# Splitting each 128x1024 unit of weights with one cast and one subtraction instead of two halves each

## The chip, the cores and the metric

The kernel runs on one core of one Trainium2 chip. The metric is the device time of one execution in microseconds: 1812.07 us is the median of three runs (1810.32, 1812.13 and 1812.07). All times below are microseconds unless marked ns. The engines are PE (TensorE's matmuls) and PEld (its weight loads), DVE (VectorE), ACT (ScalarE), POOL (GpSimd) and SP, which here only issues DMAs.

## The reference

The program is the forward pass of two stacked blocks on one sequence of 256 tokens with 1024 features. The first block has two layers: a SwiGLU feed-forward, a mixer, and a second feed-forward, each followed by a layer norm of the residual. Its mixer is a gated linear recurrence (RG-LRU) in layer 0 and a dilated attention with keys and values shared from the layer before in layer 1. The second block puts 16 meta tokens in front (272 tokens) and has two layers of a hybrid mixer (retention, pooling and a forgetting attention) and a SwiGLU feed-forward.

```
x = layer_norm(ALPHA*x + 0.5*swiglu(x, w_in, w_out))
x = layer_norm(ALPHA*x + mixer(x))          # rglru_block or dilated_attention
x = layer_norm(ALPHA*x + 0.5*swiglu(x, w_in2, w_out2))
...
h = layer_norm_2(ALPHA*h + mix @ w_out)     # second block, twice
h = layer_norm_2(ALPHA*h + (silu(h@w1) * (h@w3)) @ w2)
```

What matters here is that almost all of the time goes into matrix products of a 1024- to 2816-long input with large fp32 weights, each weight used once.

## The kernel before, in words

Activations lie transposed in SBUF: 128 features on the partitions, 256 or 272 tokens on the free axis. Every weight matrix is cut into 128x128 tiles, and the tiles lie in DRAM in the order in which the program uses them, eight to a unit of 128x1024 fp32 numbers (512 KB): 537 units. A product of full precision is made of three matmuls in the fast format fp32r (`mm3`, matmul at L147): weight and input are each split into a high part, rounded to fp32r, and a low part, the difference; the three matmuls are high x high, high x low and low x high. So each unit feeds 24 matmuls.

Three steps bring a unit to PE. `_dma` (L77) loads it into a raw buffer (five of them) from the queue of SP. `_hi` (L87) makes the high part on ACT, as two casts of 128x512. `_lo` (L99) makes the low part as two subtractions of 128x512, raw minus high; they run on DVE, but on POOL while `lo_pool` is set, which is so in the recurrence (`rg`). High and low parts have seven buffers each. `w` hands out the tiles one by one, and at the first tile of each unit `pump(2)` splits up to two more units, never more than six units ahead of the one in use.

DVE and ACT have other work between the splits: the evacuation of PSUM (L441 to L443 in the feed-forward), the splits of activations (L159 and L160), the residual and what the next norm needs (L252, L211, L215, L198), the norm itself (L272 to L300), and the mixers' own vector work: convolution, scans and gates in `rg` (L508 to L566), softmaxes, and the chain of the forget gates in the second block's mixer (L840 to L855). Norms are covered by `filler`: the first output tiles of the next stage are computed from the input that is not yet normalised, and put right afterwards.

The order of the instructions on each engine is fixed when the program is built. A scheduler walks the instructions in the order in which the code emits them, gives the engine that is free in its own estimate of time the earliest one that is ready, and assigns the semaphores. Blocks under `high_priority(offset=100)` (the residual, the statistics, the norm) are ranked as if emitted 100 instructions earlier. On the chip each engine then works through its list strictly in order. At the start, `body` splits the first two units between the splits of the first input tiles.

Of the kernel before, what the change touches and what calls it, by code (L numbers as in the profile page):

```python
# [57 lines left out]
class Builder:  # L58
# [12 lines left out]

    # ---------------------------------------------------------------- weights
    def _dma(self):
# [4 lines left out]
        self.raws[u] = raw  # L78

    def _hi(self):  # L80
        u = self.nhi
        while self.ndma < min(u + RAWS, N_UNIT):
            self._dma()
        self.nhi += 1
        hi = self.p_w.tile([128, UNIT * 128], F32R, tag="whi", name="whi")
        for q in range(0, UNIT * 128, 512):
            self.nc.scalar.copy(hi[:, q:q + 512], self.raws[u][:, q:q + 512])  # L87
        self.his[u] = hi

    def _lo(self, pool=False):  # L90
        u = self.nlo
        while self.nhi <= u:
            self._hi()
        self.nlo += 1
        lo = self.p_w.tile([128, UNIT * 128], F32R, tag="wlo", name="wlo")
        eng = self.nc.gpsimd if pool or self.lo_pool else self.nc.vector
        r, h = self.raws.pop(u), self.his[u].bitcast(F32)
        for q in range(0, UNIT * 128, 512):
            eng.tensor_tensor(lo[:, q:q + 512], r[:, q:q + 512], h[:, q:q + 512], op=ALU.subtract)  # L99
        self.los[u] = lo  # L100

    def pump(self, n, pool=False):
        """Splits up to n more units of weights, the high parts one unit ahead of the low parts."""
        u = self.used // UNIT
        while n > 0 and self.nlo < min(u + LOOK, N_UNIT):
            if self.nhi < min(self.nlo + 2, N_UNIT):
                self._hi()
            self._lo(pool)
            n -= 1
# [18 lines left out]

    # ---------------------------------------------------------------- helpers
    def bank(self, n=1, hold=None):  # L130
        """The next free psum bank (or aligned pair, or three in a row); a held one is skipped until it is let go."""
        b = self.bank_ptr
        for _ in range(16):
            b %= 8
            if (n == 2 and b % 2) or b + n > 8 or any(b + i in h for h in self.held.values() for i in range(n)):
                b += 1
                continue
            break
        else:
            raise AssertionError("no free bank")  # L140
        self.bank_ptr = (b + n) % 8
        if hold is not None:
            self.held[hold] = range(b, b + n)
        return self.ps[:, b, :] if n == 1 else self.ps[:, b:b + n, :]
# [23 lines left out]

    # ---------------------------------------------------------------- layer norm
    def ln_begin(self, ln, N):  # L170
# [3 lines left out]
    def emb_begin(self):  # L174
        """The columns and the meta tokens that the norm of all tokens adds to the first block's last one."""
        nc = self.nc
        nc.scalar.copy(self.gh[:, :, LTOT:LTOT + 4], self.exh.bitcast(F32))
        nc.scalar.copy(self.gl[:, :, LTOT:LTOT + 4], self.exl.bitcast(F32))
        t = self.p_ln.tile([128, LTOT], F32, tag="nt", name="nt", bufs=3)[:, 0:KD * META]
        t = t.rearrange("p (k n) -> p k n", k=KD)  # L180
        nc.vector.tensor_tensor(t, self.xf[:, :, 0:META], self.ex[:, :, 2:3].to_broadcast([128, KD, META]), op=ALU.mult)
        self.split(self.gh[:, :, 0:META], self.gl[:, :, 0:META], t)

    def sums(self, m, N, off, sq, eng, eng2=None):
        """Running sums of x and x^2 over the feature tiles."""
        a = self.acc
# [16 lines left out]
    def fold_to(self, m, ln, N):  # L203
        """Factor and columns of the next stage's first input."""
        if ln == LN_EMB - 1:
# [12 lines left out]
    def prep(self, ms, ln, N, off, fold=True):  # L218
        """What the next norm needs of the feature tiles ms, which end together."""
        nc = self.nc  # L220
# [23 lines left out]
    def scale_in(self, m, ln, N, off):  # L244
        """x <- x g, once the sums have what they need of it."""
        x = self.xf[:, m, off:off + N]
# [8 lines left out]
    def stats(self, N, eps, tail=None, dst=None):  # L255
        """Mean and deviation of every token from the running sums; tail: the last tile's share comes on top."""
        nc = self.nc
# [22 lines left out]
    def table(self, func, after):  # L280
        """Has ScalarE load the table set of func ahead of its use."""
        self.nc.scalar.activation(self.dummy, after, func)

    def norm(self, ln, N, off):
        """Normalises all feature tiles, software-pipelined over VectorE and ScalarE."""
        nc = self.nc
# [16 lines left out]
    def norm_last(self, ln, N, off, i, eng, rstd, nm):  # L303
        """Normalises a feature tile that scale_in has been over."""
        nc = self.nc
# [16 lines left out]
    def filler(self, specs, ln, N, off, eps, pool, tag="fv", bufs=2, when=(1, 3)):  # L322
        """First output tiles of a stage, from the not yet normalised input."""
        n = len(specs)
# [15 lines left out]
    def emb_filler(self, specs, eps_in, eps, pool, tag):  # L340
        """The first output tiles of the second block, from the first block's last sums: two norms are still to come.
        The first one is of the tokens without the meta tokens, the second one of all."""
        nc = self.nc
# [45 lines left out]
    def group(self, specs, N, kout=False, mid=None):  # L389
        """Output tiles in pairs from the normalised input; returns one [128, 2, N] psum view per pair.  # L390
        mid: what is emitted after the first half."""
        shared = 2 * N <= 512
# [15 lines left out]
    def out_proj(self, K, hh, hl, spec, coef, ln, N, off, fold, waves, korder=None, hooks={}):  # L408
        """x <- x + coef * (h @ W), in waves of output tiles; hooks: what is emitted amid the first wave."""
        if ln == LN_EMB - 1:  # L410
# [20 lines left out]

    # ---------------------------------------------------------------- feed forward
    def ffn(self, sg, su, so, coef, ln_in, ln_out, N, off, eps_in, fold_out=True):
# [24 lines left out]

    # ---------------------------------------------------------------- RG-LRU
    def rg(self, ln_in, ln_out, eps):  # L460
# [140 lines left out]

    # ---------------------------------------------------------------- shared keys and values
    def kv(self, ln_in, eps):
# [32 lines left out]

    # ---------------------------------------------------------------- dilated attention
    def attn(self, ln_in, ln_out, eps):
        nc = self.nc
        N, off = SEQ, META  # L640
        with self.tc.tile_pool(name="attn", bufs=1) as p:
# [20 lines left out]
            def put(pr, g, src):  # L662
                """High part of a head's queries in its own half of the partitions, low part in the other one."""
                for e in range(2):
# [69 lines left out]
            def step(n=1):  # L734
                """Head i's scores while the heads before it are a stage further each."""
                for _ in range(n):
# [35 lines left out]

    # ---------------------------------------------------------------- second block's mixer
    def mixer(self, l, ln_in, ln_out, eps, eps_in=None):
# [4 lines left out]
        with self.tc.tile_pool(name="mix", bufs=1) as p:  # L779
# [26 lines left out]

            # ---- projections of the forgetting attention
            six = l == 0
# [28 lines left out]
            nc.gpsimd.memset(one, 1.0)  # L837
            # log sigmoid of the forget logits and its running sum
            with self.tc.high_priority(offset=PRIO):
# [54 lines left out]

            # ---- forgetting attention, one head at a time
            S, DEN, PT, O = {}, {}, {}, {}
# [82 lines left out]

            # ---- retention  # L980
            SM = p.tile([128, N], F32, name="SM")
# [98 lines left out]

            # ---- multi-scale pooling
            ua = {}
# [36 lines left out]

            # ---- order of work  # L1120
            def pair(a, b, mid=None):
# [81 lines left out]

    # ---------------------------------------------------------------- whole program
    def dump(self, N, off):
# [109 lines left out]
def constants():  # L1315
    """Tables that depend on shapes alone."""
    f8 = np.float64
# [49 lines left out]
def feat(a):  # L1367
    """[..., n*128] -> [128, ... * n]"""
    a = np.asarray(a)
    return np.ascontiguousarray(a.reshape(-1, 128).T)  # L1370


def lay_out(inp, plan):
    """Inputs rearranged for the program: no arithmetic, only order (and zero padding)."""
    r = {}
# [66 lines left out]
```

## Time and profile before

| | |
|---|---|
| runs | 1810.32, 1812.13, 1812.07; median 1812.07 |
| profiled execution | span 1813.3 from first to last instruction; the page gives no time of its own outside of it |
| busy PE / PEld / DVE / ACT / POOL | 1741.0 / 1675.4 / 1272.0 / 1032.6 / 230.0 |
| casts of the weights, ACT L87 | 1074 of 128x512, 615.5 busy |
| subtractions, DVE L99 | 1032 of 128x512, 685.7 busy |
| subtractions, POOL L99 | 42 of 128x512, 63.3 busy |

Busy time is the union of an engine's instructions; "idle" names the time just before an instruction and what ended it. In a timeline, consecutive instructions of one kind are merged: start, length, count. The chain of waits goes back from the last instruction to what released each step, so an engine's share in it is the time that this engine held up the end. [...]

### The profile page before, as it was taken

Reading aid. Unit: us, or ns where it says so; the run is one execution under the profiler, and the core shown is the slowest. Engines: PE = TensorE matmul, PEld = TensorE weight load, DVE = VectorE, ACT = ScalarE, POOL = GpSimd, SP = SyncE. Lnnn points to the kernel's source line nnn. Section 1 sums busy time; section 2 is a strip of 40 time slices with the busy share of each in tenths; the row PEclk is TensorE's granted clock in tenths of the full one; section 3 lists DMA queues with packets and bytes.
Section 4 is the critical chain, followed back from the end, with each engine's and each line's share of the span. In section 5 each row is a group of like instructions: output and inputs, shape, how many; then the busy total and the mean of one; then the engine's idle time right before and its main releaser. Section 6 shows DMA issues by size and latency. Waiting matters only on the chain.

```text
span 1813.3 us, 34554 instructions
## 1 busy us (share of the span) xinstructions
PE 1741.0 (96%) x13558; PEld 1675.4 (92%) x13558; DVE 1272.0 (70%) x2399; ACT 1032.6 (57%) x2090; POOL 230.0 (13%) x266
## 2 busy tenths in 40 slices
PE   8999978999999999999999999799999999999997
PEld 8999977999999999977789999788999998899996
DVE  6666899966676666756668666897965569687653
ACT  6444666744465444644547445775744457575443
POOL 0001355000100001201120001320200030120001
PEclk9999988999999999968999999999999999999999
DMA  8555435565548555732225555433365554246550
GB/s 292 185 187 186 145 105 168 170 209 186 182 156 280 186 187 186 208 118 82 82 85 179 188 183 184 154 106 106 118 208 176 177 188 152 83 129 223 186 186 35
DMA packets 85372, 296.80 MB, mean 164 GB/s; under 512 B 10892, under 2 KB 14232, under 8 KB 84696
## 3 DMA queue, kind: packets, MB, share of 16 engines
q1 hardware_dynamic: 80216, 283.79, 47.1%
q0 software_dynamic: 1424, 7.38, 1.3%
q10 hardware_dynamic: 3568, 3.41, 0.6%
q8 instruction: 106, 1.74, 0.4%
q14 instruction: 58, 0.48, 0.1%
HBM read 290.24 MB, written 4.19 MB: 162 GB/s over the span
## 4 chain that ended last, share of the span: by engine, by line
PE 82%; DVE 11%; ACT 3%; issue 2%; DMA 1%; POOL 1%; DVEq 0%; SPq 0%; POOLq 0%; ACTq 0%
PE ps L147 81%; DVE wlo L99 3%; DMA KL<-kl 1%; PE ps L155 1%; ACT whi L87 1%; DVE uc L510 0%; DVE gl L300 0%; DVE T L561 0%; DVE xf L252 0%; POOL wlo L99 0%; DVE nt L291 0%; DVE gl L215 0%; POOL acc L193 0%; DVE rstd L277 0%; DMA raw<-in_wst_dram 0%
## 5 line engine op out<-in xcount | busy, mean ns | idle before, releaser
L87 ACT CAST whi<-raw 128x512 fp32r<-128x512 f32 x1074 | 615.5, 617 | 525.7 <-issue 311.0
L99 DVE TENSOR_TENSOR wlo<-raw,whi 128x512 fp32r<-128x512 f32 x1032 | 685.7, 701 | 321.5 <-ACT whi L87 319.6
L147 PE MATMUL ps<-gh,whi 128*128 128x256 f32 (+3 forms) x2864 | 829.0, 290 | 19.6 <-ACT gh L297 8.7
L147 PE MATMUL ps<-gl,whi 128*128 128x256 f32 (+3 forms) x2864 | 823.3, 288 | 1.0 <-DVE gl L300 1.0
L147 PE MATMUL ps<-gh,wlo 128*128 128x256 f32 (+3 forms) x2864 | 818.4, 286 | 0.0
L147 PEld LDWEIGHTS ps<-gh,whi 128*128 128x128 f32 x2864 | 549.3, 192 | 27.2 <-ACT gh L297 9.3
L147 PEld LDWEIGHTS ps<-gl,whi 128*128 128x128 f32 x2864 | 550.9, 192 | 5.9 <-issue 2.6
L147 PEld LDWEIGHTS ps<-gh,wlo 128*128 128x128 f32 x2864 | 551.1, 192 | 1.3 <-issue 0.7
L147 PE MATMUL ps<-hh,wlo 128*128 128x256 f32 (+1 forms) x1056 | 298.0, 282 | 0.0
L147 PE MATMUL ps<-hh,whi 128*128 128x256 f32 (+1 forms) x1056 | 297.9, 282 | 0.0
L147 PE MATMUL ps<-hl,whi 128*128 128x256 f32 (+1 forms) x1056 | 297.7, 282 | 0.0
L147 PEld LDWEIGHTS ps<-hl,whi 128*128 128x128 f32 x1056 | 199.0, 188 | 0.0
L147 PEld LDWEIGHTS ps<-hh,whi 128*128 128x128 f32 x1056 | 199.0, 188 | 0.0
L147 PEld LDWEIGHTS ps<-hh,wlo 128*128 128x128 f32 x1056 | 198.8, 188 | 0.0
L193 POOL TENSOR_TENSOR acc<-xf 128x256 f32<-128x256 f32 (+1 forms) x10 | 7.6, 759 | 1060.7 <-DVE xf L252 907.7
L443 DVE TENSOR_TENSOR th<-th,ps 128x512 f32<-128x512 f32 (+1 forms) x62 | 42.9, 691 | 54.3 <-PE ps L147 54.3
L193 POOL TENSOR_TENSOR acc<-acc,xf 128x256 f32<-128x256 f32 (+1 forms) x50 | 45.5, 910 | 192.3 <-DVE xf L252 177.3
L99 POOL TENSOR_TENSOR wlo<-raw,whi 128x512 fp32r<-128x512 f32 x42 | 63.3, 1536 | 46.2 <-ACT whi L87 46.2
L252 DVE SCALAR_TENSOR_TENSOR xf<-ps,xf 128x256 f32<-128x256 f32 (+1 forms) x80 | 32.9, 422 | 41.1 <-PE ps L147 40.9
L198 ACT ACTIVATE sq<-xf 128x256 f32<-128x256 f32 (+1 forms) x88 | 35.6, 410 | 44.6 <-DVE xf L252 36.8
L211 ACT ACTIVATE gh<-xf,prm 128x256 fp32r<-128x256 f32 (+1 forms) x64 | 32.1, 508 | 47.9 <-DVE xf L252 47.9
L215 DVE SCALAR_TENSOR_TENSOR gl<-xf,prm,gh 128x256 fp32r<-128x256 f32 (+1 forms) x64 | 44.5, 706 | 11.0 <-ACT gh L211 11.0
(330 smaller groups left out, 1927.8 us busy)
## 6 DMA issues: line engine op xcount, KB each, us to landing
raw<-in_wst_dram SPq DMA_DIRECT2D x537, 512.0 KB, 3.4
cst<-in_c_mix_dram POOLq DMA_DIRECT2D x2, 1138.0 KB, 5.5
KH<-kh POOLq DMA_DIRECT2D x4, 512.0 KB, 13.7
kh<-kh ACTq DMA_DIRECT2D x4, 256.0 KB, 4.8
kl<-kl ACTq DMA_DIRECT2D x4, 256.0 KB, 6.6
vsc<-kt ACTq DMA_DIRECT2D x4, 256.0 KB, 6.0
KL<-kl POOLq DMA_DIRECT2D x1, 1024.0 KB, 21.5
Vt<-vsc POOLq DMA_DIRECT2D x1, 1024.0 KB, 23.9
```

The costliest lines, as they stand in the source:

```text
L87: self.nc.scalar.copy(hi[:, q:q + 512], self.raws[u][:, q:q + 512])
L99: eng.tensor_tensor(lo[:, q:q + 512], r[:, q:q + 512], h[:, q:q + 512], op=ALU.subtract)
L147: self.nc.tensor.matmul(out, lhsT, rhs, start=start, stop=stop, skip_group_check=True)
L155: self.nc.tensor.matmul(out, in_, self.ident[0:n, 0:n], start=True, stop=True, is_transpose=True, skip_group_check=True)
L193: eng.tensor_tensor(a[:, 0, 0:N], x0, x, op=ALU.add)
L198: self.nc.scalar.activation(sq[:, 0:N], self.xf[:, m, off:off + N], AF.Square)
L211: return self.nc.scalar.activation(self.gh[:, m, c], self.xf[:, m, off:off + N], AF.Copy, scale=g)
L215: return self.nc.vector.scalar_tensor_tensor(self.gl[:, m, c], self.xf[:, m, off:off + N], g, self.gh[:, m, c].bitcast(F32), op0=ALU.mult, ...
L252: self.nc.vector.scalar_tensor_tensor(x, banks[m][:, 0:N], coef, x, op0=ALU.mult, op1=ALU.add)
L443: nc.vector.tensor_tensor(th, th, pu, op=ALU.mult)
```

## The change

A new function `piece` gives the width of one instruction of the split: 512 columns for the first three units, 1024 for all others. `_hi` and `_lo` step by it. Docstrings and comments are taken out too, which changes no instruction.

```diff
+    def piece(self, u):
+
+        return 512 if u < 3 else UNIT * 128
+
     def _hi(self):
...
-        for q in range(0, UNIT * 128, 512):
-            self.nc.scalar.copy(hi[:, q:q + 512], self.raws[u][:, q:q + 512])
+        n = self.piece(u)
+        for q in range(0, UNIT * 128, n):
+            self.nc.scalar.copy(hi[:, q:q + n], self.raws[u][:, q:q + n])
...
     def _lo(self, pool=False):
...
-        for q in range(0, UNIT * 128, 512):
-            eng.tensor_tensor(lo[:, q:q + 512], r[:, q:q + 512], h[:, q:q + 512], op=ALU.subtract)
+        n = self.piece(u)
+        for q in range(0, UNIT * 128, n):
+            eng.tensor_tensor(lo[:, q:q + n], r[:, q:q + n], h[:, q:q + n], op=ALU.subtract)
```

## Rows read from the trace of the kernel before

**Rows 1.** The page's first part: busy time, share of the span, instructions.
```profile
PE 1741.0 (96%) x13558; PEld 1675.4 (92%) x13558; DVE 1272.0 (70%) x2399; ACT 1032.6 (57%) x2090; POOL 230.0 (13%) x266
```

**Rows 2.** Stages: length; busy of PE, PEld, DVE, ACT, POOL; clock, DMA share, GB/s.
```profile
204.00:311.00 107.00, 84.82 (x650) 82.58 (x648) 100.83 (x157) 72.85 (x143) 63.27 (x42) 0.90 0.39 129
311.00:518.00 207.00, 207.00 (x1741) 206.24 (x1741) 146.16 (x259) 116.34 (x229) 10.29 (x12) 1.00 0.57 189
...
777.00:907.00 130.00, 130.00 (x631) 100.36 (x632) 79.72 (x196) 60.06 (x129) 18.04 (x26) 0.83 0.24 79
...
1145.00:1290.00 145.00, 128.59 (x888) 116.93 (x889) 125.95 (x304) 102.24 (x244) 35.06 (x48) 0.94 0.35 115
...
1490.00:1610.00 120.00, 113.41 (x846) 105.65 (x844) 97.69 (x236) 80.09 (x199) 24.93 (x38) 0.99 0.40 133
...
1802.00:1813.30 11.30, 0.00 (x0) 0.00 (x0) 7.92 (x16) 6.08 (x11) 1.67 (x2) 0.64 0.27 93
```

**Rows 3.** Timeline of PE: start, length, instruction; in brackets the idle time before.
```profile
7.05 0.58 PE L147 MATMUL ps<-gh,whi 128*128 128x256 f32 x1 [7.05 <-ACT whi L87]
...
235.82 0.77 PE L147 MATMUL ps<-uch,whi 128*128 128x256 f32 x2 [8.91 <-DVE uch L515]
...
300.87 0.58 PE L147 MATMUL ps<-yl,whi 128*128 128x256 f32 x1 [6.89 <-DVE yl L160]
```

**Rows 4.** The chain of waits: its shares by line, and two of its pieces.
```profile
by line: PE ps L147 80.7%; DVE wlo L99 2.5%; issue 1.9%; DMA KL<-kl 1.2%; PE ps L155 0.9%; ACT whi L87 0.9%; DVE uc L510 0.4%; DVE gl L300 0.4%; DVE T L561 0.4%; DVE xf L252 0.4%; POOL wlo L99 0.3%; DVE nt L291 0.3%; DVE gl L215 0.3%; POOL 
...
1199.74 0.70 DVE wlo L99
...
1538.97 1.19 DVE wlo L99
```

**Rows 5.** Groups by shape: count, busy and mean ns of one, idle before.
```profile
L99 DVE TENSOR_TENSOR wlo<-raw,whi 128x512 fp32r<-128x512 f32 x1032 | 685.7, 701 | 321.5 <-ACT whi L87 319.6
L87 ACT CAST whi<-raw 128x512 fp32r<-128x512 f32 x1074 | 615.5, 617 | 525.7 <-issue 311.0 <-PE ps L147 196.8 <-DMA raw<-in_wst_dram 12.3
...
L160 DVE TENSOR_TENSOR hl<-th,hh 128x512 fp32r<-128x512 f32 x55 | 37.6, 684 | 0.8 <-ACT hh L159 0.7
...
L292 DVE TENSOR_TENSOR nt<-nt,nm 128x256 f32<-128x256 f32 x48 | 19.1, 416 | 0.0
...
L297 ACT CAST gh<-xf 128x256 fp32r<-128x256 f32 x48 | 18.0, 398 | 0.0
```

**Rows 6.** Timeline of DVE: splits in a row, and between a chain's steps.
```profile
28.62 3.69 DVE L99 TENSOR_TENSOR wlo<-raw,whi 128x512 fp32r<-128x512 f32 x6
...
1518.09 0.69 DVE L99 TENSOR_TENSOR wlo<-raw,whi 128x512 fp32r<-128x512 f32 x1
1518.82 0.44 DVE L852 SCALAR_TENSOR_TENSOR cp<-cp,cw 6x272 f32<-6x272 f32 x1
1519.29 0.69 DVE L99 TENSOR_TENSOR wlo<-raw,whi 128x512 fp32r<-128x512 f32 x1
...
1522.39 0.44 DVE L852 SCALAR_TENSOR_TENSOR cp<-cp,cw 6x272 f32<-6x272 f32 x1
1522.86 0.44 DVE L989 TENSOR_TENSOR ru<-ps,cst 128x272 f32<-128x272 f32 x1
```

**Rows 7.** Timeline of ACT: four casts in a row.
```profile
309.69 2.17 ACT L87 CAST whi<-raw 128x512 fp32r<-128x512 f32 x4
```

**Rows 8.** Timeline of POOL: subtractions in `rg`, and the fastest 128x256 addition.
```profile
230.24 2.53 POOL L99 TENSOR_TENSOR wlo<-raw,whi 128x512 fp32r<-128x512 f32 x2 [0.22 <-ACT whi L87]
...
289.32 12.62 POOL L99 TENSOR_TENSOR wlo<-raw,whi 128x512 fp32r<-128x512 f32 x8 [2.14 <-ACT whi L87]
...
1607.06 0.73 POOL L193 TENSOR_TENSOR acc<-acc,xf 128x256 f32<-128x256 f32 x1 [0.76 <-DVE xf L252]
```

**Rows 9.** Timeline of DVE in `rg`: scans and the split of the recurrence's output.
```profile
264.83 1.26 DVE L561 TENSOR_TENSOR_SCAN T<-R,V 128x256 f32<-128x256 f32 x2
...
292.80 3.40 DVE L561 TENSOR_TENSOR_SCAN T<-R,V 128x256 f32<-128x256 f32 x2
...
299.13 1.68 DVE L160 TENSOR_TENSOR yl<-gy,yh 128x512 fp32r<-128x512 f32 x1
```

## Prediction, before the changed kernel ran

> **What bounds the kernel now.** I read the page's busy times first, then a table by stage, then the idle times of PE, then the chain of waits, and last the groups of the split by shape with the timelines around them. The reader is to see that PE is busy for 1741.0 of the span of 1813.3 us [rows 1], so 72.3 us are idle. Of these, 7.05 lie ahead of the first matmul [rows 3] and 11.3 behind the last one [rows 2]: 54 us of gaps are left in the middle, and no shorter split can give back more than these and the slow clock that follows some of them. The table by stage shows where they lie. A feed-forward stage has none: PE is busy for 207.00 of 207.00 us at clock 1.00, with DVE at 146 and ACT at 116. The recurrence has 22 us of gaps with DVE busy for 100.8 of 107, the two hybrid mixers 16 and 7 us with DVE busy for 126 of 145 and 98 of 120. The attention has no gap in the stretch shown, but a clock of 0.83 [rows 2]. So PE sets the pace over most of the span, and DVE's list in the mixers and at their borders. The chain agrees: matmuls hold 80.7% of it, the subtractions on DVE 2.5%, the casts on ACT 0.9% and the subtractions on POOL 0.3% [rows 4]. These shares of 1813.3 are 45, 16 and 5 us, and they are what the change can act on.
>
> **The change part by part.** Units 3 to 536 go from two instructions to one for each part: of 1074 casts 534 go, of 1032 subtractions on DVE 513, of 42 on POOL 21 [rows 2, 5]. The same elements are worked on, so what goes is the fixed part of an instruction, and what comes is a longer instruction.
>
> DVE: 128x512 takes 684 ns where little is in its way (activations, L160) and 128x256 takes 416 [rows 5], so 512 more columns cost 2 x 268 = 536 and a 128x1024 takes 1.22 us (an estimate). Six halves in a row take 3.69 us, that is (3.69 - 0.69) / 5 = 0.60 from start to start, 0.085 less than one lasts [rows 6]; a whole unit then takes 1.135 against 1.20, and saves 0.07. Where halves stand alone between the steps of a dependent chain, two of them take 2 x 0.72 (1518.09 to 1518.82 is 0.73), a whole one 1.25, and 0.19 is saved. 45 us of chain at 0.64 are about 70 halves, 35 units; between 35 x 0.07 = 2.5 and 35 x 0.19 = 6.7 I take the middle, -4.6 us.
>
> ACT: 617 ns for 512 and 398 for 256 [rows 5] give 617 + 2 x 219 = 1.055 us for a unit; four halves take 2.17, so 0.52 from start to start [rows 7], 0.10 less than one lasts. A unit goes from 1.04 to 0.955: 0.08 saved. 16 us of chain are some 15 units: -1.2 us.
>
> POOL: one half takes 1.265 (2.53 for two), 128x256 at its fastest 0.73 [rows 8], so a unit takes 1.265 + 2 x 0.535 = 2.33 where two halves take 2.53: 0.20 saved, 4.2 us over 21 units. Whether that reaches PE depends on DVE. In a run of eight halves one takes 12.62 / 8 = 1.58 [rows 8], and DVE's scans beside it 1.70 each instead of 0.63 [rows 9]: the two engines take turns, one DVE instruction to one of POOL, with 1.58 - 1.265 = 0.31 of each turn DVE's alone. With whole units a turn is 2.33 + 0.31 = 2.64, and in it one DVE instruction gets through; its partner follows at 0.60. So 3.24 for two of DVE and a unit, against 3.16 now: +0.08 a unit. At the end of the stretch at 289 it is worse: the seventh DVE instruction, the split of yl that PE waits for after 6.89 us of idleness [rows 3, 9], comes now after 7 x 1.58 = 11.1 us, ahead of the eighth half; with four whole units it comes after 4 x 2.64 + 3 x 0.60 = 12.4, 1.3 later. Best case -4.2, worst 21 x 0.08 + 1.3 = +3.0; I take 0, as the gap at 235.82 lies behind all its halves and the one at 300.87 amid them.
>
> [...]
>
> Length itself: an instruction that falls due while a split is running waits for the rest of it, and the rest of a unit can be 0.53 longer than that of a half on DVE, 0.44 on ACT. Among the 195 longest pieces of the chain 13 are lone halves on DVE of 0.6 us and more, the first at 1199.74, the last at 1538.97 [rows 4]; three are lone casts. At least 0 (the scheduler finds gaps twice as long, or puts the unit where its two halves were), at most 13 x 0.53 + 3 x 0.44 = 8.2; I take a fifth, +1.5, because the lone halves of rows 6 stand in a chain of many equal steps where half as many units take half as many places.
>
> At no cost: the low part must now wait for the whole high part, 0.44 us later, and the first matmul of a unit for all of it, 0.5 more. The six units of lookahead hide it (24 matmuls of a unit take 24 x 0.119 = 2.9 us, from 207.00 / 1741 [rows 2]); without that cover it would be 1 us a unit where PE waits. The first three units keep their halves, so the 7.05 us ahead of the first matmul stay. The loads are the same in size, queue and number. The feed-forward's savings on DVE and ACT become idle time of engines that PE outlasts.
>
> Sum: -4.6 - 1.2 + 0 + 1.5 = -4.3 us. It is made against the span of 1813.3; the page gives nothing around it, and the span lies 1.2 above the median of the runs, so I take the difference from the median: 1812.07 - 4.3 = 1807.8. Where a gap on the chain shortens, the next thing late is the table load and square root of the norm or PE itself.
>
> **The rivals.**
> *Hidden anyway.* The engines' lists are written anew, and PE's gaps are set by the norm and the dependent chains, with splits merely standing there. For it: the chain step of rows 6 goes on at 0.47 where no half stands between, so the halves fill only part of the wait. Against: DVE is busy for 94% of the recurrence [rows 2]. Time 1812, between 1810 and 1813.
> [...]
> *Longer splits in the way of short steps.* Slower: in the mixers, between 1145 and 1610, units stand ahead of due steps of norm and softmax. If all 13 lone halves and 3 casts grow, +8.2; with the savings kept that is 1812.07 - 5.8 + 8.2 = 1814.5, with the savings lost too (off the chain in the new order) 1820; I put it at 1817. It decides from 11 lone halves on (5.8 / 0.53). For it: 13 are on the chain. Against: each unit takes away one of two such places.
> *A new order in the attention.* Its 130 us run at clock 0.83 [rows 2]; at full clock that stretch would lose up to 0.17 x 130 = 22 us, and a different order of PE's instructions moves some of that, 5 either way.
>
> **How the numbers follow.** Forecast 0.50, hidden 0.18, POOL's turns 0.10, longer splits 0.17, attention 0.05. About 0.2%, 3.6 us, is what a measurement of this kernel can tell from no change. Of the forecast 0.41 lies beyond it, 0.07 within, 0.02 on the other side; of the hidden case 0.15 is within and 0.03 slower; of POOL's turns 0.08 and 0.02; of the attention 0.04 faster and 0.01 slower; the longer splits are slower. Faster 0.45, same 0.30, slower 0.25. The forecast's own range is 1802 to 1811 (terms at -6.7 - 1.2 - 4.2 + 0 = -12.1 and -2.5 - 1.2 + 3.0 + 0 = -0.7, pulled in a little); the whole range is 1799 to 1818, with the rival of longer splits at its upper end and the attention's 5 at its lower one.
>
> **What would show it.** After, the page should have 540 casts (534 of 128x1024 at about 1.05 us), 519 subtractions on DVE (513 at about 1.22) and 21 on POOL near 2.3 to 2.7; DVE busy down by 513 x (2 x 0.685 - 1.22) = 77 us, ACT by 534 x 0.18 = 96. The feed-forward stages should keep their length. The gaps at 235.82 and 300.87 should keep 8 to 10 and 6 to 9 us; the mixers should be shorter by 2 to 5 us in all. [...] The forecast is wrong if the mixers' gaps grow, or if a feed-forward stage changes.

## The result and the profile after

The changed kernel is slower: 1820.22 us in the median of six runs, against 1810.61 for six runs of the kernel before on the same chip, a ratio of 1.0066 with a 95% interval of 1.0045 to 1.0086 (the ratio of the medians alone is 1.0053, that of the means 1.0062; both lie in the interval). That is 12 us, 8 to 16, on the other side of no change than the forecast of 1807.8 and above its whole range of 1799 to 1818. The profiled execution of after has a span of 1818.5 and a time of 1820.3.

The first lines to read are busy time and the groups of the split (count, busy, mean ns of one, idle before).

```profile
PE 1736.4 (95%) x13558; PEld 1670.7 (92%) x13558; DVE 1235.8 (68%) x1886; ACT 984.9 (54%) x1556; POOL 231.5 (13%) x245
...
L105 DVE TENSOR_TENSOR wlo<-raw,whi 128x1024 fp32r<-128x1024 f32 (+1 forms) x519 | 633.6, 1225 | 368.1 <-ACT whi L92 366.9
L92 ACT CAST whi<-raw 128x1024 fp32r<-128x1024 f32 (+1 forms) x540 | 560.1, 1042 | 556.4 <-PE ps L153 457.6
...
L105 POOL TENSOR_TENSOR wlo<-raw,whi 128x1024 fp32r<-128x1024 f32 x21 | 53.1, 2548 | 63.3 <-ACT whi L92 63.3
```

Against [rows 1, 5] every engine that splits weights has done its splits in less time: DVE's subtractions fell from 685.7 to 633.6, ACT's casts from 615.5 to 560.1, POOL's subtractions from 63.3 to 53.1. The durations were estimated well (1.22 and 1.055 us forecast, 1.225 and 1.042 measured). So this is a case in which the work became less and the time longer. DVE's whole busy time fell only by 36, less than its splits' 52: other instructions on it became longer.

The table by stage shows where (length; busy of PE, PEld, DVE, ACT, POOL; clock, as the share of full speed granted to PE; DMA share, GB/s). The first two rows are the recurrence's stage, from the first matmul of the statistics ahead of it to the first one behind it, first in after, then in before.

```profile
199.47:337.00 137.53, 111.56 (x836) 108.39 (x834) 126.56 (x197) 87.10 (x143) 53.12 (x21) 0.90 0.41 135
```
```profile
199.62:329.61 129.99, 107.81 (x835) 104.89 (x834) 123.31 (x211) 89.41 (x178) 63.27 (x42) 0.92 0.43 140
```

This stage alone is 7.5 us longer. PE's timeline in it answers to [rows 3] (in brackets the idle time before an instruction and what ended it):

```profile
215.78 1.01 PE L153 MATMUL ps<-gh,whi 128*128 128x256 f32 x3 [6.25 <-ACT gh L303]
...
237.55 0.77 PE L153 MATMUL ps<-uch,whi 128*128 128x256 f32 x2 [7.18 <-DVE uch L521]
...
288.79 0.39 PE L153 MATMUL ps<-gh,whi 128*128 128x256 f32 x1 [1.88 <-ACT whi L92]
...
291.22 0.58 PE L153 MATMUL ps<-gh,wlo 128*128 128x256 f32 x1 [1.93 <-POOL wlo L105]
...
310.02 0.58 PE L153 MATMUL ps<-yh,whi 128*128 128x256 f32 x1 [3.19 <-ACT yh L165]
...
312.58 0.58 PE L153 MATMUL ps<-yl,whi 128*128 128x256 f32 x1 [1.98 <-DVE yl L166]
```

The two gaps that the forecast spoke of are there, 7.18 for 8.91 and, in pieces, 3.19 and 1.98 for 6.89. New are the 6.25 at the norm, 2.19 in before, and two waits for a split, which before did not have in this stage. The norm's wait in before, and in e2 below, where POOL keeps its halves and only ACT and DVE have wholes:

```profile
211.88 0.50 PE L147 MATMUL ps<-gh,whi 128*128 128x256 f32 x2 [2.19 <-ACT gh L297]
```
```profile
213.21 0.80 PE L147 MATMUL ps<-gh,whi 128*128 128x256 f32 x2 [5.08 <-ACT gh L297]
```

All gaps over 0.3 us add up to 25.7 in after and 21.8 in before. PE is also busy for 3.75 us longer with 836 records for 835, and the reason stands behind the gaps (busy time and clock of two stretches of after):

```profile
284.80:289.80 5.00, 2.62 (x20) 0.97 0.08 31
289.80:294.80 5.00, 3.58 (x16) 0.50 0.37 113
```

In the first of these PE is busy for 2.62 of 5.00 us at a clock of 0.97; in the second the granted clock is 0.50, and matmuls that start every 0.12 us elsewhere in the stage start every 0.21. By the starts in PE's timeline 56 matmuls of this stage went at that pace in before and 82 in after, so 26 x 0.095 = 2.5 us are the clock's and 3.9 the gaps'; the other 1.1 of the 7.5 lie in shorter delays.

The rest of the kernel, stage by stage: the two feed-forward stages behind the gate are 1.3 and 0.7 longer and the last one 1.2, the first hybrid mixer is 1.5 longer and the second 1.9 shorter, the attention 4.1 shorter.

The chain of waits answers to [rows 4]: DVE's subtractions hold more of it, not less (2.9% for 2.5%), ACT's casts too (1.2% for 0.9%). That "issue" (time in which the profile shows nothing that was waited for) went from 1.9% to 5.3% is no loss: 47.5 us of it lie between 880 and 932 us, in the attention, where the chain of after follows POOL's steps (L711) and that of before PE's, and that stage is not longer.

```profile
by line: PE ps L153 76.0%; issue 5.3%; DVE wlo L105 2.9%; ACT whi L92 1.2%; DMA raw<-in_wst_dram 1.0%; PE ps L161 0.7%; DVE T L567 0.7%; DVE nt L297 0.7%; DVE uc L516 0.6%; DVE nt L298 0.5%; DVE rstd L283 0.4%; DVE gl L306 0.4%; POOL t L711
```

### The profile page after: what moved, and what is told of

Same layout as the page of the kernel before. It is cut to its first block, busy times and chain, and to the rows that moved or that the text cites. A ratio compares the mean times of both kernels' runs of the same rounds, so it can differ in the third digit from the quotient of the medians.

```text
span 1818.5 us, 33480 instructions
## 1 busy us (share of the span) xinstructions
PE 1736.4 (95%) x13558; PEld 1670.7 (92%) x13558; DVE 1235.8 (68%) x1886; ACT 984.9 (54%) x1556; POOL 231.5 (13%) x245
## 4 chain that ended last, share of the span: by engine, by line
PE 77%; DVE 12%; issue 5%; ACT 3%; DMA 1%; POOL 1%; SPq 0%; DVEq 0%; POOLq 0%; ACTq 0%
PE ps L153 76%; DVE wlo L105 3%; ACT whi L92 1%; DMA raw<-in_wst_dram 1%; PE ps L161 1%; DVE T L567 1%; DVE nt L297 1%; DVE uc L516 1%; DVE nt L298 1%; DVE rstd L283 0%; DVE gl L306 0%; POOL t L711 0%; DVE xf L258 0%; POOL acc L199 0%; DVE T L564 0%
## 5 line engine op out<-in xcount | busy, mean ns | idle before, releaser
L105 DVE TENSOR_TENSOR wlo<-raw,whi 128x1024 fp32r<-128x1024 f32 (+1 forms) x519 | 633.6, 1225 | 368.1 <-ACT whi L92 366.9
L92 ACT CAST whi<-raw 128x1024 fp32r<-128x1024 f32 (+1 forms) x540 | 560.1, 1042 | 556.4 <-PE ps L153 457.6
L153 PEld LDWEIGHTS ps<-hh,wlo 128*128 128x128 f32 x1056 | 198.8, 188 | 0.0
L199 POOL TENSOR_TENSOR acc<-acc,xf 128x256 f32<-128x256 f32 (+1 forms) x50 | 53.1, 1061 | 182.1 <-DVE xf L258 167.6
L258 DVE SCALAR_TENSOR_TENSOR xf<-ps,xf 128x256 f32<-128x256 f32 (+1 forms) x80 | 32.8, 422 | 53.1 <-PE ps L153 53.0
L105 POOL TENSOR_TENSOR wlo<-raw,whi 128x1024 fp32r<-128x1024 f32 x21 | 53.1, 2548 | 63.3 <-ACT whi L92 63.3
L221 DVE SCALAR_TENSOR_TENSOR gl<-xf,prm,gh 128x256 fp32r<-128x256 f32 (+1 forms) x64 | 45.2, 717 | 11.2 <-ACT gh L217 11.1
```

What stands on the lines that cost most here:

```text
L92: self.nc.scalar.copy(hi[:, q:q + n], self.raws[u][:, q:q + n])
L105: eng.tensor_tensor(lo[:, q:q + n], r[:, q:q + n], h[:, q:q + n], op=ALU.subtract)
L153: self.nc.tensor.matmul(out, lhsT, rhs, start=start, stop=stop, skip_group_check=True)
L199: eng.tensor_tensor(a[:, 0, 0:N], x0, x, op=ALU.add)
L221: return self.nc.vector.scalar_tensor_tensor(self.gl[:, m, c], self.xf[:, m, off:off + N], g, self.gh[:, m, c].bitcast(F32), op0=ALU.mult, ...
L258: self.nc.vector.scalar_tensor_tensor(x, banks[m][:, 0:N], coef, x, op0=ALU.mult, op1=ALU.add)
```

## The experiments

Twelve kernels in three groups; each is timed against the kernel before on the same chip. Line numbers in them are those of before. The widths became functions of the unit and the engine:

```diff
-        for q in range(0, UNIT * 128, 512):
-            self.nc.scalar.copy(hi[:, q:q + 512], self.raws[u][:, q:q + 512])
+        for q in range(0, UNIT * 128, self.hw(u)):
+            self.nc.scalar.copy(hi[:, q:q + self.hw(u)], self.raws[u][:, q:q + self.hw(u)])
...
+Builder.hw = lambda self, u: 512 if u < 3 else HW
+Builder.lw = lambda self, u, eng: 512 if u < 3 else LP if eng is self.nc.gpsimd else LD
```

with the same edit in `_lo`. HW is then ACT's width, LD is DVE's, LP is POOL's; before is 512, 512, 512 and the change 1024, 1024, 1024. A change of LP alone leaves the order of the instructions on every engine as it was; changes of HW and LD bring a new one.

The results in one table. "Gate" is the change of the recurrence's stage against 129.99 of before. "gl" is the time from the statistics' first matmul behind that stage to the first split of the normalised input (L300), and "attention" the length of the attention's stage; these three are from one profiled execution each.

| kernel | widths | ratio, 95% interval | gate | gl | attention |
|---|---|---|---|---|---|
| before | 512, 512, 512 | 1 | 0 | 9.13 | 202.6 |
| changed | 1024, 1024, 1024 | 1.0066 (1.0045 to 1.0086) | +7.5 | 11.68 | 198.5 |
| e1 | 512, 512, 1024 | 1.0042 (1.0027 to 1.0057) | +6.7 | 9.12 | 199.1 |
| e2 | 1024, 1024, 512 | 1.0051 (1.0035 to 1.0067) | +2.6 | 11.74 | 196.6 |
| e3 | 1024, 1024, 1024 | 1.0073 (1.0053 to 1.0093) | +7.4 | 11.68 | 198.6 |
| e4 | 512, 512, 256 | 0.9990 (0.9971 to 1.0008) | -1.2 | 9.17 | 190.0 |
| e5 | 512, 1024, 512 | 0.9985 (0.9967 to 1.0004) | +2.3 | 10.27 | 196.6 |
| e6 | 1024, 512, 512 | 1.0029 (1.0010 to 1.0047) | +2.5 | 10.77 | 199.9 |
| e7 | wholes in mid feed-forward only | 1.0001 (0.9979 to 1.0023) | -0.9 | 9.16 | 193.3 |
| e8 | 256 on DVE and POOL elsewhere | 1.0004 (0.9984 to 1.0023) | -4.0 | 8.40 | 205.6 |
| e9 | wholes but in mid feed-forward | 1.0051 (1.0029 to 1.0072) | +3.7 | 11.69 | 198.8 |
| e10 | 256 on DVE and POOL in the gate | 0.9991 (0.9972 to 1.0010) | -4.5 | 9.26 | 194.1 |
| e11 | e10 with 256 on ACT there | 1.0003 (0.9985 to 1.0022) | -2.9 | 10.72 | 200.9 |
| e12 | e7 and e10 together | 0.9986 (0.9972 to 1.0001) | -4.4 | 9.26 | 199.8 |

Theory 1 was that DVE's short steps wait for whole instructions of POOL; rival A, that the longer instructions of ACT and DVE and their new order cost the time; rival B, that it is the attention's clock.

**e1: POOL alone whole.** LP = 1024.

> Kernel before with GpSimd's low parts alone in one 128x1024 subtraction; ScalarE's and VectorE's stay 128x512, and the order of instructions on every engine is that of before. Theory 1 (a VectorE instruction that meets a GpSimd one waits to its end, so the chain's small steps are caught for up to 2.5 us where it was 1.27): ratio 1.003 to 1.006, the loss in the recurrent gate's stage (start of the kernel to 330 us about 7 us later than in before), small VectorE steps of over 2 us beside GpSimd's turns. Rival A (the longer ScalarE and VectorE instructions, and the new order they bring, cost the time): ratio 1.000 within 0.001, gate stage as in before. Rival B (the loss is the attention's granted clock): no loss in the gate's stage, any difference between 680 and 960 us.

Measured: 1.0042, 1818.77 us, the gate stage 6.7 longer. Theory 1 holds for this part, and rival A does not explain it, since order and widths of ACT and DVE are those of before. As the order is the same, one can read line by line how a longer wait on DVE reaches PE. First before, then e1 (start, length, count, idle before):

```profile
272.08 3.30 DVE L561 TENSOR_TENSOR_SCAN T<-R,V 128x256 f32<-128x256 f32 x2
275.31 1.44 DVE L547 TENSOR_SCALAR gy<-gy 128x512 f32<-128x512 f32 x1
...
279.63 1.78 DVE L537 SCALAR_TENSOR_TENSOR V<-tin,uc 128x512 f32<-128x512 f32 x1
...
277.57 0.63 ACT L549 ACTIVATE gy<-gy 128x512 f32<-128x512 f32 x1 [3.37 <-DVE gy L548]
...
270.82 10.03 POOL L99 TENSOR_TENSOR wlo<-raw,whi 128x512 fp32r<-128x512 f32 x6 [7.40 <-ACT whi L87]
```
```profile
274.79 5.51 DVE L561 TENSOR_TENSOR_SCAN T<-R,V 128x256 f32<-128x256 f32 x2
280.22 2.54 DVE L547 TENSOR_SCALAR gy<-gy 128x512 f32<-128x512 f32 x1
...
283.59 0.63 ACT L549 ACTIVATE gy<-gy 128x512 f32<-128x512 f32 x1 [6.68 <-DVE gy L548]
...
274.10 8.38 POOL L99 TENSOR_TENSOR wlo<-raw,whi 128x1024 fp32r<-128x1024 f32 x3 [8.58 <-ACT whi L87]
...
287.88 0.39 PE L147 MATMUL ps<-gh,whi 128*128 128x256 f32 x1 [1.28 <-ACT whi L87]
...
291.37 0.56 PE L147 MATMUL ps<-gh,wlo 128*128 128x256 f32 x1 [2.99 <-POOL wlo L99]
```

Both times POOL subtracts three units. In before its six halves catch four DVE steps: two scans and the first step of a gelu, which last 4.74 us in all, and the L537 step of 1.78; in e1 its three wholes catch the same first three, which last 8.05. Over the whole stage, take as caught a DVE step that overlaps a POOL subtraction and lasts over 0.3 us longer than the shortest of its line and shape in the same trace. Then the 42 halves of before catch 31 steps and make them 30.6 us longer, and the 21 wholes of e1 catch 20 and make them 36.6 longer. So there are not half as many caught steps, as the forecast's turns had it, but two thirds, each losing nearly twice as much: not every half meets a step that it can hold, nearly every whole does. ACT's activation of that gelu then waits 6.68 instead of 3.37, the casts behind it in ACT's list start 3 us later, POOL's next subtraction waits for them, and PE for both. PE's gaps over 0.3 us are 1.8 longer in this stage than in before, and 96 matmuls start at the lower clock's pace for 56, which is 3.8 us: more of the 6.7 is the clock behind the gaps than the gaps.

**e2: the change with POOL at halves.**

```diff
-Builder.lw = lambda self, u, eng: 512 if u < 3 else 1024
+Builder.lw = lambda self, u, eng: 512 if u < 3 else 512 if eng is self.nc.gpsimd else 1024
```

> Changed kernel with GpSimd's low parts back in two 128x512 subtractions; the order of instructions on the other engines is that of the changed kernel. Theory 1: the loss is gone, ratio to before 0.997 to 1.001 (the forecast's gain of 5 us less what the rest costs). Rival A: still slower, 1.004 to 1.008. Rival B: anything, with the gate's stage as in the changed kernel.

Measured: 1.0051, 1816.7 us. Theory 1 alone is too little: POOL's half being back, the gate stage falls from +7.5 to +2.6, but the kernel stays slower by 9 us (6 to 12). Rival A holds for this part. Most of the gate's +2.6 is the norm at its start: PE's waits there add up to 5.8 for 2.7 in before. So there are two causes, and each was now taken by itself.

**e3: the change again**, all three at 1024, as the mark.

> The changed kernel again, on the same chip as the two others, as the mark: all theories 1.005 to 1.008, the gate's stage ending about 7 us later than in before.

Measured: 1.0073, gate +7.4; every stage within 0.2 us of the first profile of after.

**e4: POOL in quarters**, LP = 256.

> Kernel before with GpSimd's low parts in four 128x256 subtractions each, all else and the order as in before. Theory 1: the wait of a caught VectorE step falls to at most 0.65 us; the gate's stage is 2 to 4 us shorter than in before, ratio 0.997 to 0.999, unless GpSimd's turns grow by the overhead of twice as many instructions. Rival A and B: 1.000 within 0.001.

Measured: 0.9990 with 1 in the interval; the gate stage 1.2 shorter, less than expected. With e1 and before this makes three sizes of one instruction. The three steps shown under e1 take here 2.19 and 0.89, together 3.08 against 4.74 and 8.05. Smaller steps show it best, such as a run of 128x10 operations in `rg` (start, length). Beside quarters:

```profile
206.69 0.70 DVE L492 SCALAR_TENSOR_TENSOR e<-e,z 128x10 f32<-128x10 f32 x1
...
210.50 0.16 DVE L492 SCALAR_TENSOR_TENSOR e<-e,z 128x10 f32<-128x10 f32 x1
...
270.21 2.19 DVE L561 TENSOR_TENSOR_SCAN T<-R,V 128x256 f32<-128x256 f32 x2
272.32 0.89 DVE L547 TENSOR_SCALAR gy<-gy 128x512 f32<-128x512 f32 x1
...
206.36 3.86 POOL L99 TENSOR_TENSOR wlo<-raw,whi 128x256 fp32r<-128x256 f32 x4 [15.01 <-ACT whi L87]
```

in before, beside halves:

```profile
207.82 1.26 DVE L492 SCALAR_TENSOR_TENSOR e<-e,z 128x10 f32<-128x10 f32 x1
209.34 1.23 DVE L492 SCALAR_TENSOR_TENSOR e<-e,z 128x10 f32<-128x10 f32 x1
...
207.48 3.06 POOL L99 TENSOR_TENSOR wlo<-raw,whi 128x512 fp32r<-128x512 f32 x2 [15.02 <-ACT whi L87]
```

and in after, beside wholes:

```profile
209.10 2.32 DVE L498 SCALAR_TENSOR_TENSOR e<-e,z 128x10 f32<-128x10 f32 x1
211.68 2.30 DVE L498 SCALAR_TENSOR_TENSOR e<-e,z 128x10 f32<-128x10 f32 x1
...
208.95 5.00 POOL L105 TENSOR_TENSOR wlo<-raw,whi 128x1024 fp32r<-128x1024 f32 x2 [16.57 <-ACT whi L92]
```

The reader is to see that one and the same operation takes 0.16 with POOL idle and 0.70, 1.25 and 2.31 beside quarters, halves and wholes, of which one takes POOL 0.97, 1.53 and 2.50 in these rows (3.86 / 4, 3.06 / 2 and 5.00 / 2): the step lasts 0.2 to 0.3 us less than one instruction of POOL.

For the second cause, theory 2 was that a whole unit on DVE stands longer between a norm's or a mixer's short steps; its rival, that ACT's longer casts do it.

**e5: DVE alone whole**, LD = 1024.

> Kernel before with VectorE's low parts alone in one 128x1024 subtraction; ScalarE and GpSimd stay at halves. Theory 2 (a whole unit stands between the short VectorE steps of a norm or mixer and makes each wait up to 0.5 us longer): ratio 1.002 to 1.005, feed-forward stages after a norm 1 us longer each, the gate's stage 1 to 3 us longer. Rival (the longer casts on ScalarE do it): 0.999 to 1.001, those stages as in before.

Measured: 0.9985 with 1 just inside the interval. Theory 2 falls in its time: nothing is lost, though the gate is 2.3 longer (PE's gaps in it are 1.0 shorter, but 91 matmuls for 56 start at the lower clock's pace). This count does not follow the gaps alone: in e4, whose gaps are 5.1 shorter than those of before, it is 73. Its expectation of feed-forward stages 1 us longer fell too: the one behind the gate kept its length (188.71 for 188.63).

**e6: ACT alone whole**, HW = 1024.

> Kernel before with ScalarE's casts alone in one 128x1024 each. Theory 2: 1.000 to 1.002, since ScalarE is the least loaded and few of its casts stand on the chain. Rival (the casts do it): 1.002 to 1.005, with the feed-forward stages after a norm 1 us longer.

Measured: 1.0029, 5 us slower (2 to 9): the rival holds in its time. In the gate (+2.5) PE's gaps are 2.8 longer; it waits for a cast, and longer for the split of the recurrence's output (8.60, for ACT's part; 6.89 in before, for DVE's):

```profile
283.79 0.39 PE L147 MATMUL ps<-gh,whi 128*128 128x256 f32 x1 [1.94 <-ACT whi L87]
...
303.81 0.58 PE L147 MATMUL ps<-yh,whi 128*128 128x256 f32 x1 [8.60 <-ACT yh L159]
```

The first mixer with the statistics ahead of it is 1.7 longer at 142.6, but the kernels that have before's widths there (before, e1, e4, e7, e10 to e12) take 140.6 to 142.1 for it, so that is hardly more than this scatter. The feed-forward stage behind the gate is here too within 0.2 us of before, while in e2, with both, it is 1.3 longer, and the next one 0.65. The column "gl" says why. Of the norm behind the gate, DVE's timeline in after (first the statistics on PE, last PE's wait):

```profile
337.00 0.70 PE L153 MATMUL ps<-acc,ones 128*128 128x512 f32 x1
...
337.85 2.36 DVE L105 TENSOR_TENSOR wlo<-raw,whi 128x1024 fp32r<-128x1024 f32 x2 [0.45 <-ACT whi L92]
340.13 0.42 DVE L279 SCALAR_TENSOR_TENSOR var<-ps,var 128x256 f32<-128x256 f32 x1
340.55 1.23 DVE L105 TENSOR_TENSOR wlo<-raw,whi 128x1024 fp32r<-128x1024 f32 x1
341.69 0.29 DVE L280 TENSOR_SCALAR var<-var 128x256 f32<-128x256 f32 x1
342.46 1.75 DVE L283 RECIPROCAL rstd<-var 128x256 f32<-128x256 f32 x1 [0.48 <-ACT var L281]
344.13 1.16 DVE L105 TENSOR_TENSOR wlo<-raw,whi 128x1024 fp32r<-128x1024 f32 x1
...
348.68 0.42 DVE L306 TENSOR_TENSOR gl<-xf,gh 128x256 fp32r<-128x256 f32 x1
...
349.15 0.39 PE L153 MATMUL ps<-gl,whi 128*128 128x256 f32 x1 [0.43 <-DVE gl L306]
```

and in before:

```profile
329.61 0.70 PE L147 MATMUL ps<-acc,ones 128*128 128x512 f32 x1
...
331.85 0.41 DVE L273 SCALAR_TENSOR_TENSOR var<-ps,var 128x256 f32<-128x256 f32 x1
332.19 0.68 DVE L99 TENSOR_TENSOR wlo<-raw,whi 128x512 fp32r<-128x512 f32 x1
332.79 0.28 DVE L274 TENSOR_SCALAR var<-var 128x256 f32<-128x256 f32 x1
...
338.74 0.41 DVE L300 TENSOR_TENSOR gl<-xf,gh 128x256 fp32r<-128x256 f32 x1
...
340.80 0.28 PE L147 MATMUL ps<-gl,whi 128*128 128x256 f32 x1
```

Between several steps of the norm stands a split, now of 1.23 where it was 0.68. From the statistics to gl DVE does five wholes in after and seven halves in before, so it is also more splitting that stands ahead of gl. In before gl begins 9.13 after the statistics and PE, busy with the next stage's first tiles, comes for it at 340.80, 11.2 after them: 2 us of slack, less the 0.41 that the step lasts. Wholes on DVE use 1.14 of it (10.27), on ACT 1.64 (10.77), and either alone is hidden; together 2.55 (11.68) are more than there is, and PE waits. This wait and the slower starts around it cost 0.8 of that stage's 1.3; the rest builds up over the next thousand matmuls without a gap, and its cause is open.

The same holds at other norms. Some 12 to 14 us behind the statistics at 518, 752, 955 and 1610 us of before, PE waits 0.3 to 0.7 us for gl in after, e2 and e3, and not in before, e5 and e6. At the norm ahead of the gate, where PE waits in before already, its waits add up to 2.7 in before, 2.5 in e5, 2.5 in e6, but 5.8 in e2. What stays open is whether the width or the new order does it: no run changes the width on ACT or DVE and keeps the order.

**e7: wholes only where no norm and no mixer is due.**

```diff
+ST = any(s + 14 <= u < s + 60 for s in (0, 101, 183, 281, 376, 471))
+HW = LD = 1024 if ST else 512
```

> ScalarE and VectorE take whole units only in the middle of each of the six feed-forward stages (46 of their 66 units), halves elsewhere; GpSimd halves. Theory 2: ratio 0.999 to 1.001 and every stage within 0.5 us of before, because no short step that TensorE waits for runs there. Rival (whole units cost wherever they are, by contention or by the high part's later end): 1.002 to 1.005, the feed-forward stages longer in their middle.

Measured: 1.0001. The stages behind the gate, 330 to 752 us of before, are within 0.1 of their length. The three later feed-forward stages are 1.5, 1.2 and 1.6 shorter, but the last two are so by as much in e4, with halves, and the first by 1.4 in e10, so this is not the wholes' doing. Wholes cost nothing in the middle of the feed-forward, and bring nothing. The profiled execution lies low (span 1797.9) mostly by its attention of 193.3, in which no width differs from before.

**e9: the complement**, wholes everywhere else: `HW = LD = 512 if ST else 1024`.

> The complement of steady_whole: ScalarE and VectorE take whole units everywhere but in the middle of the six feed-forward stages; GpSimd halves. If the loss of the whole casts and subtractions comes from where short steps of a norm, the gate's stage or a mixer are due: the whole loss of the kernel with GpSimd at halves is here, ratio 1.003 to 1.006, the norm after the gate's stage ending 11.5 to 12 us after its statistics as there (9.1 in before). If the loss depends on how many whole units there are, wherever: about half of it, 1.001 to 1.003.

Measured: 1.0051, as in e2, with gl at 11.69, the next two feed-forward stages 1.3 and 0.6 longer, the gate +3.7, and the first mixer with the statistics ahead of it +4.3. So the loss of ACT's and DVE's wholes lies in 258 of the 537 units, where short steps are due, as far as the timing can tell (the interval of e7 reaches 1.0023): their place counts and not their number.

**e8: finer instead of coarser.** LP = 256 and `LD = 512 if ST else 256`.

> The other direction: GpSimd's low parts in quarters, and VectorE's in quarters for the units outside the middle of the feed-forward stages; ScalarE at halves. Theories 1 and 2 if waits of short steps are what counts: 0.996 to 0.999, the gate's stage 2 to 4 us shorter and the feed-forward stages no longer. Rival (the fixed part of an instruction counts more from here on, VectorE being busy for 87% of the mixers): 1.000 to 1.003, the mixers longer.

Measured: 1.0004. The gate gains the expected 4.0 and gl comes at 8.40, but no gain of the kernel shows. The first mixer with the statistics ahead of it is 1.2 longer, as the rival has it, but so it is in e11, with before's widths there; so the rival is not shown by it. The attention is 205.6 in this execution.

**e10: finer in the gate only.** In the gate's stage (units 66 to 106) POOL and DVE take quarters, elsewhere all is as in before: LP = 256, `LD = 256 if 66 <= u < 107 else 512`.

> [...] If waits behind a split are what sets this stage: the stage 3 to 5 us shorter than in before, all others as before, ratio 0.997 to 0.998. If the fixed part of twice as many instructions eats it: 1.000 and the stage within 1.5 us.

Measured: the gate 4.5 shorter, at 125.51, with PE at a clock of 0.95:

```profile
199.20:324.71 125.51, 108.00 (x836) 105.17 (x834) 120.14 (x239) 90.14 (x178) 81.89 (x84) 0.95 0.44 144
```

but the ratio is 0.9991 (0.9972 to 1.0010): the stage's gain is in the trace, the ratio misses the expected 0.997 to 0.998, and the timing does not tell it from nothing.

**e11: e10 with ACT in quarters there**, `HW = 256 if 66 <= u < 107 else 512`.

> As the kernel with finer splits in the gate's stage, with ScalarE's casts in quarters there too. If a cast in the way of ScalarE's short steps counts as it seems to between halves and wholes (2.5 us in this stage): another 0 to 2 us shorter, ratio 0.996 to 0.998. If ScalarE's fixed part counts: equal or longer by up to 1 us.

Measured: 1.0003, the gate 1.6 longer than in e10 and the next stage 1.6 longer. This misses the expected gain. The next stage loses its 1.6 at its start: PE waits 1.88 for the statistics' input and goes on at a start every 0.21. That the fixed part of ACT's instructions did it would fit the second expectation but is not shown; by the ratio e11 is not told from e10.

**e12: e7 and e10 together.** `HW = 1024 if ST else 512`, `LD = 1024 if ST else 256 if 66 <= u < 107 else 512`, LP = 256.

> Each width where it fits: whole units on ScalarE and VectorE in the middle of the feed-forward stages, quarters on GpSimd and VectorE in the gate's stage, halves elsewhere. Both gains and losses add: equal to the kernel with finer splits in the gate's stage alone, 0.997 to 0.998, as whole units in the feed-forward stages are worth nothing there.

Measured: 0.9986 (0.9972 to 1.0001), 1805.24 us in the median. That is the lowest median here, short of the expected 0.997 to 0.998, level with e5 by its ratio, and not quite told from before.

**Rival B.** The attention's stage took from 190.0 to 205.6 us in these profiles, and its granted clock goes with that: over 130 us of the stage it was 0.93 in e4 (190.0), 0.88 in after (198.5), 0.83 in before (202.6) and 0.82 in e8 (205.6). In e4, whose instructions and widths there are all those of before, the stage has a clock of 0.94 where before has 0.87 (first before, then e4):

```profile
752.28:954.84 202.56, 195.81 (x1075) 157.16 (x1075) 136.23 (x317) 106.88 (x231) 36.44 (x51) 0.87 0.34 107
```
```profile
749.97:939.99 190.02, 184.20 (x1074) 147.16 (x1075) 136.31 (x317) 106.60 (x231) 36.03 (x51) 0.94 0.36 114
```

So this stage differs by some 12.5 us between executions with nothing changed in it, and all runs of before by 16 (1799.1 to 1815.3 in the last group of runs). The loss does not need it: without the attention the profiled after is 9.3 longer than the profiled before, and e3 9.2. Whether wholes make the attention itself a little longer on average, single executions cannot tell: with before's widths it took 190.0 to 202.6, in after, e2, e3, e6 and e9 196.6 to 199.9. The rest of the kernel scatters too: without the attention e2 is 4.6 longer and e9 11.6, at the same ratio. That it also hides gains of 4 us from a timing, as in e10, is likely and not shown. What sets its clock stays open.

## Why the prediction was wrong, step by step

**POOL, taken as 0, bounds -4.2 to +3.0.** This is the first step that failed. Measured alone it is +7.6 us (4.9 to 10.3, from 1.0042 of 1810.45), and 6.7 of it in the one stage where POOL splits. The working had one DVE instruction get through in each turn of POOL, so that half as many turns would hold up half as many. In the trace 42 halves caught 31 steps and 21 wholes caught 20 (e1), and each caught step lost 1.8 us instead of 1.0. The gelu's steps L548 and L550, whose second input lies in PSUM, lasted 0.66 to 0.69 beside POOL and without it in before and after, so some halves in before held up nothing. The bound of +3.0 came from the same run of eight halves and left out what follows: the casts behind the waiting activation, PE's wait for them, and the clock behind the gaps. For POOL's turns, at a chance of 0.10, no run shows a price of +3.0: e1 shows +7.6 in its place, and beside wholes scans lasted up to 2.81 us in after, 0.66 by themselves.

**ACT, -1.2.** The sign was wrong: alone it is +5.2 (2 to 9). The saved part of each cast is real (busy time on that line fell by 55), but it went into idle time of an engine that was busy for 57% [rows 1]. How a cast delays a short step is seen at the norm behind the gate: its first step on ACT begins 1.68 after the statistics in after, 1.34 in before, with a cast of 1.04 in the way instead of 0.62. In e6, with wholes on ACT alone, the delay there is hidden. It costs in the gate, where PE's gaps grew by 2.8; that casts stand in the way there in the same manner is argued, not shown step by step, and the rest of the 5.2 is not located.

**DVE, -4.6.** Alone -2.7 (-6.0 to +0.7), which with a share of the length term agrees. The busy time was to fall by 77 and fell by 52 on these lines (ACT's by 96 and fell by 55), since the means of a half in [rows 5] count the overlap of neighbours twice: 685.7 / 1032 is 0.66, not 0.685, and for ACT 615.5 / 1074 is 0.57.

**Length itself, +1.5, bounds 0 to 8.2.** It was sized by the lone splits that stood on the chain of before. That misses the steps which were not on that chain but close to it. It also took half as many units to take half as many places; at the norm behind the gate seven halves became five wholes. The norm behind the gate had 2 us of slack; two growths of 1.14 and 1.64 that are free one by one ran over it together. So the feed-forward stages became longer by 1.3 and 0.65, where the forecast let them keep their length. The forecast's own range left this term's bound of 8.2 out; with it the upper bounds, -2.5 - 1.2 + 3.0 + 8.2, give 1819.6. The rival "longer splits in the way of short steps" put the place in the mixers and the time at 1817; e2, with POOL apart, has 1816.7, so it was nearly right in size at a chance of 0.17. That is luck in part, for the place was another: in e2 the first mixer is 1.5 longer, near its scatter, and the second 1.9 shorter; what grew were the waits at the norms.

**At no cost: the later end of a high part.** Six units of lookahead hide it in the feed-forward (e7). In the gate PE waits 1.88 for a cast and 1.93 for a subtraction of POOL that it did not wait for before. In e1 they are 1.28 and 2.99 with casts in halves, so they come in part from the delays behind POOL. In e6, with POOL in halves, they are 1.94 and 0.85, so ACT's wholes alone bring them too, and taking this term at no cost was wrong in the gate.

**The sum.** 9.2 for ACT and DVE together and 7.6 for POOL make 16.8; the change measured 12 (8 to 16) and 13 (10 to 17). In the gate the parts are 2.6 and 6.7 and the whole 7.5, so there they overlap in part, probably because a step held up by one had waited for the other anyway. The right answer to this change would have been a loss by POOL and one by the longer splits of ACT and DVE at once.

## What to carry to other kernels

In these runs the length of an instruction off the critical path was a price on the short dependent steps that met it: on its own engine (gl came 1.14 us later with wholes on DVE, 1.64 with wholes on ACT) and, for DVE and POOL, on the other one (a scan took up to 1.13 us more beside POOL's halves, 2.15 beside its wholes). Busy time saved on an engine that was not the bound bought nothing back (ACT's casts fell by 55 us in after; e6, with wholes on ACT alone, was 5 us slower). So size fillers by the place: coarse in stretches where only PE counts (though it brought nothing here), fine where a chain of short steps runs, and price each chain by its slack, adding up all changes before asking whether it is used up. When a change takes several engines at once, expect terms that are free one at a time and not together.

## What the runs showed of the hardware

A VectorE operation on 128x10 elements, 0.16 us by itself, took 0.70, 1.25 and 2.31 us beside GpSimd subtractions of 256, 512 and 1024 columns: that is 0.54, 1.09 and 2.15 more than by itself. A scan over 256 columns, 0.66 by itself, took up to 1.79 beside halves and 2.81 beside wholes, 1.13 and 2.15 more, so 256 columns waited as long as 10. Not every VectorE step was longer beside GpSimd: those at L548 and L550 (L554 and L556 in after), with one of two inputs in PSUM, took 0.66 to 0.69 beside it and without it, in before and in after. GpSimd's own busy time for the same 21 units goes the other way, 53.1 as wholes (2.55 each) and 63.3 as halves; as quarters it was 79.0 (e4), so that shorter waits of VectorE are paid for in GpSimd's time. And one stage with the same instructions took 190.0 and 202.6 us in two executions (e4 and before), with a granted clock of 0.94 and 0.87.
